# Log-sum-exp on one core: regrouping the exponentials and row sums of the first five loads

## The chip, the cores and the metric

The kernel runs on one core of a Trainium2 chip. The metric is the time of one execution on the device in microseconds (us), lower is better; the median of several runs is compared. The engines that matter here are ScalarE (ACT), which computes the exponentials, VectorE (DVE), which adds rows up, SyncE (SP), which issues the loads and stores, and the 16 DMA engines behind SP's queue.

## The reference

```python
x = np.random.randn(32, 512, 1024).astype(np.float32)

def reference(x):
    max_x = np.max(x, axis=-1, keepdims=True)
    return (max_x.squeeze(-1) + np.log(np.sum(np.exp(x - max_x), axis=-1))).astype(np.float32)
```

That is a stable log-sum-exp over the last axis: 16,384 rows of 1,024 numbers, 67 MB read, 64 KB written.

## The kernel before

The 16,384 rows are spread over 128 partitions, 128 rows in each. "A row" below means one row in each partition, 1,024 float32 columns (0.5 MB over all partitions). The kernel takes the exponential without subtracting the maximum, sums it and takes the logarithm; a check at the end (the matmuls into `count`, L143 to L251) decides whether the sums stayed in a safe range, and only if not does a second, slower pass run (L258 to L301).

The data come in 18 loads of the sizes in the table `LOADS` (L17), from 16 rows down to 0.375. They go into a ring of 48 rows (`RING`) in the on-chip memory, one after the other; when a load would run past the end, the position goes back to 0. Loads 1 to 3 fill the 48 places, load 4 (16 rows) overwrites load 1, load 5 (13.5) begins at place 16, load 6 (12.5) at 29.5, and load 7 (9) begins again at 0.

The function `load` issues a load on SP's queue (L126). Before it does, SP waits for every earlier user of the places that it overwrites; `users` holds those with the engine and the count at which they are done, and an entry that has been waited for is dropped. SP issues in the order of the loads. The loads carry no wait for each other, so several can be under way in the queue.

Each load has a string of operations that work through its rows in order:

- `Rn`: one exponential over n rows on ACT, in place (L192), then one row sum of these n rows on DVE (`reduce_sum`, L196).
- `Tn`: one exponential over n rows on ACT (L192), then on DVE for each row one `scalar_tensor_tensor` that adds its two halves and accumulates the sum (L204).
- `A`: one row on ACT alone, exponential and sum in one instruction with an accumulator (L181).
- `Y`, `Z`: the two pieces of the last row, on ACT with an accumulator (L170).

The last operation of a load also takes the exponential of the part of a row that the load ends with, so that the next load finds it done (`upto`, L190).

ACT waits for a load to land and then runs its operations without a wait for DVE. DVE waits for each exponential. The only wait of ACT for DVE before the tail is at row 119 (`LATE`), before the early logarithm (L219) over rows 0 to 111, which by then have been summed. Both engines run in the order in which the program is written.

Of the kernel before, what the change touches and what calls it, by code (L numbers as in the profile page):

```python
# [14 lines left out]


LOADS = [  # L17
    (16, "R8 R7 A"), (16, "R8 R7 T1"), (16, "R8 R8"), (16, "R6 R5 R5"), (13.5, "R5 R4 T4"),
    (12.5, "R7 R6"), (9, "A A A A A A A A A"), (7.5, "R3 R2 R2"), (5.5, "R4 T2"),
    (4.625, "T4"), (3.3125, "T3"), (2.4375, "T3"), (1.8125, "T2"), (1.3125, "T1"), (0.9375, "T1"),  # L20
    (0.5625, "T1"), (0.625, "Y"), (0.375, "Z"),
# [341 lines left out]
```

## Time and profile before

| | |
|---|---|
| median of 3 runs | 162.66 us (162.47 to 162.76) |
| the profiled execution | 163.04 us, of which the span of the profile is 161.7 us |
| busy: DMA queue / DVE / ACT | 97.2% / 73% / 72% of the span |
| read from HBM | 67.11 MB, 415 GB/s over the span |

A row of the profile's groups reads: line, engine, operation, what it writes <- what it reads with shapes, count | busy us in all, mean ns of one | idle time of the engine just before these, and what ended most of it. A row of a timeline reads: start, duration (both us from the start of the span), engine, line, operation, count when several that follow each other are merged, and in brackets the idle time before it and who ended it. "SPq" is SP's queue of instructions, where the issue of a load is seen. A row of the DMA issues gives the size in KB and the time from the issue to the landing.

### The profile page before, as it was taken

What the parts mean: (1) busy time and instruction counts of PE and PEld (TensorE: products, weight loads), DVE (VectorE), ACT (ScalarE), POOL (GpSimd) and SP (SyncE); (2) the same over time, 40 slices, a digit from 0 to 9 for tenths busy, and PEclk for the clock granted to TensorE, in tenths of its full rate; (3) what the DMA queues carried; (4) which work ended last, traced back from release to release, by engine and by line L of the source; (5) the groups of instructions that cost most, each with busy time, mean ns of one, the idle gap of its engine ahead of it and who ended that gap; (6) DMA issues with size and microseconds to landing.
All of it is one profiled execution on the core that took longest, in us unless ns stands there. A gap on an engine that the chain in (4) does not pass through costs nothing.

```text
span 161.7 us, 249 instructions
## 1 busy us (share of the span) xinstructions
PE 2.1 (1%) x24; PEld 1.0 (1%) x24; DVE 117.7 (73%) x69; ACT 116.9 (72%) x55; POOL 0.2 (0%) x4
## 2 busy tenths in 40 slices
PE   0000000000000000000000000000000000000022
PEld 0000000000000000000000000000000000000011
DVE  0000000899929999399999999999399956999894
ACT  3000059980899609994299949973999999989986
POOL 0000000000000000000000000000000000000000
DMA  7997997998999899799699999998999999999990
GB/s 276 503 519 324 454 519 324 454 519 373 405 519 422 357 519 454 324 519 454 284 438 438 438 422 405 443 494 368 438 438 441 410 417 418 450 408 418 410 392 15
DMA packets 2881, 67.18 MB, mean 416 GB/s; under 512 B 576, under 2 KB 704, under 8 KB 1344
## 3 DMA queue, kind: packets, MB, share of 16 engines
q1 hardware_dynamic: 2880, 67.18, 97.2%
q14 instruction: 1, 0.01, 0.0%
HBM read 67.11 MB, written 0.07 MB: 415 GB/s over the span
## 4 chain that ended last, share of the span: by engine, by line
DMA 58%; ACT 19%; DVE 16%; another core or an unknown queue 3%; SPq 1%; issue 0%; PE 0%; DVEq 0%
DMA ring<-in_x_dram 58%; ACT ring L192 19%; DVE sumexp L196 15%; DVE ring L204 1%; SPq L126 0%; PE count L147 0%; PE count L248 0%; DVE clamped L242 0%; DVE fine L251 0%; SPq L44 0%; DVEq L44 0%
## 5 line engine op out<-in xcount | busy, mean ns | idle before, releaser
L192 ACT ACTIVATE ring<-ring 128x8192 f32<-128x8192 f32 (+18 forms) x27 | 103.6, 3891 | 41.8 <-DMA ring<-in_x_dram 41.8
L196 DVE TENSOR_REDUCE sumexp<-ring 128x8 f32<-128x8192 f32 (+6 forms) x17 | 102.9, 6107 | 39.2 <-ACT ring L192 39.2
L204 DVE SCALAR_TENSOR_TENSOR ring<-ring 128x512 f32<-128x512 f32 x22 | 14.1, 687 | 1.3 <-ACT ring L192 1.3
L181 ACT ACTIVATE ring<-ring 128x1024 f32<-128x1024 f32 x10 | 10.4, 1042 | 0.0
L114 ACT ACT_TABLE_LOAD x1 | 1.3, 1283 | 1.5 <-PEq L57 1.5
L143 PE MATMUL count<-far,bad 128*1 128x1 f32 x2 | 0.2, 164 | 153.8 <-DVE clamped L138 153.8
L181 ACT ACTIVATION_READ_ACCUMULATOR ring<-ring 128x1 f32 x10 | 1.9, 187 | 0.0
L204 DVE DVE_READ_ACCUMULATOR ring<-ring 128x1 f32 x22 | 1.8, 82 | 0.0
L147 PE MATMUL count<-sumexp,ones 128*1 128x1 f32 x20 | 1.8, 164 | 4.1 <-DVE ring L204 4.1
L170 ACT ACTIVATE last_exp<-ring 128x640 f32<-128x640 f32 (+1 forms) x2 | 1.2, 590 | 0.0
L115 DVE MEMSET ones<- 128x1 f32 x1 | 0.1, 59 | 1.5 <-PEq L57 1.5
L143 PEld LDWEIGHTS count<-far,bad 128*1 128x1 f32 x2 | 0.1, 80 | 153.8 <-DVE clamped L138 153.8
L147 PEld LDWEIGHTS count<-sumexp,ones 128*1 128x1 f32 x20 | 0.8, 81 | 5.1 <-DVE ring L204 4.9
L251 DVE TENSOR_SCALAR fine<-count 1x1 int32<-1x1 f32 x1 | 0.1, 145 | 0.5 <-PE count L147 0.5
L170 ACT ACTIVATION_READ_ACCUMULATOR last_exp<-ring 128x1 f32 x2 | 0.4, 186 | 0.0
L138 DVE SCALAR_TENSOR_TENSOR clamped<-clamped,sumexp 128x119 f32<-128x119 f32 x1 | 0.3, 282 | 0.0
L232 ACT ACTIVATE res<-sumexp 128x1 f32<-128x1 f32 x1 | 0.3, 294 | 0.0
L219 ACT ACTIVATE res<-sumexp 128x112 f32<-128x112 f32 x1 | 0.3, 279 | 0.0
L242 DVE SCALAR_TENSOR_TENSOR clamped<-sumexp 128x9 f32<-128x9 f32 x1 | 0.2, 169 | 0.1
L133 DVE TENSOR_SCALAR clamped<-sumexp 128x119 f32<-128x119 f32 x1 | 0.2, 223 | 0.0
L230 ACT ACTIVATE res<-sumexp 128x15 f32<-128x15 f32 x1 | 0.2, 198 | 0.0
L248 PE MATMUL count<-far,bad 128*1 128x1 f32 x2 | 0.2, 164 | 0.0
(8 smaller groups left out, 0.7 us busy)
## 6 DMA issues: line engine op xcount, KB each, us to landing
ring<-in_x_dram SPq DMA_DIRECT2D x1, 6912.0 KB, 31.8
ring<-in_x_dram SPq DMA_DIRECT2D x1, 6400.0 KB, 26.6
ring<-in_x_dram SPq DMA_DIRECT2D x1, 4608.0 KB, 25.2
ring<-in_x_dram SPq DMA_DIRECT2D x1, 3840.0 KB, 23.6
ring<-in_x_dram SPq DMA_DIRECT2D x1, 2816.0 KB, 26.0
ring<-in_x_dram SPq DMA_DIRECT2D x1, 2368.0 KB, 30.4
ring<-in_x_dram SPq DMA_DIRECT2D x1, 1696.0 KB, 23.1
ring<-in_x_dram SPq DMA_DIRECT2D x1, 1248.0 KB, 25.7
```

Source lines behind the costliest of these rows:

```text
L114: nc.scalar.preload_act_table_set("natural_log_exp_and_others")
L133: dve.did(nc.vector.tensor_scalar(out=clamped[:, 0:LATE], in0=sumexp[:, 0:LATE], scalar1=LOW, scalar2=HIGH, op0=ALU.max, op1=ALU.min,))
L138: dve.did(nc.vector.scalar_tensor_tensor(out=clamped[:, 0:LATE], in0=clamped[:, 0:LATE], scalar=0.0, in1=sumexp[:, 0:LATE], op0=ALU.bypass ...
L143: pe.did(nc.tensor.matmul(count, lhsT=bad[:, 0:1], rhs=far, start=True, stop=False))
L147: return pe.did(nc.tensor.matmul(count, lhsT=ones, rhs=sumexp[:, c : c + 1], **kw))
L170: at = act.did(nc.scalar.activation(out=last_exp[:, here - p : end - p], in_=ring[:, here:end], func=AF.Exp, accum_out=sumexp[:, LAST : NC ...
L181: at = act.did(nc.scalar.activation(out=v, in_=v, func=AF.Exp, accum_out=sumexp[:, c : c + 1]))
L192: at = act.did(nc.scalar.activation(out=v, in_=v, func=AF.Exp))
L196: who = (dve, dve.did(nc.vector.reduce_sum(out=sumexp[:, c : c + s], in_=rows, axis=AX.X)))
L204: who = (dve, dve.did(nc.vector.scalar_tensor_tensor(out=lo, in0=lo, scalar=1.0, in1=rows[:, r, H:d], op0=ALU.mult, op1=ALU.add, accum_out ...
L219: ln_early = act.did(nc.scalar.activation(out=res[:, 0:W], in_=sumexp[:, 0:W], func=AF.Ln))
L232: ln_last = act.did(nc.scalar.activation(out=res[:, LAST:NC], in_=sumexp[:, NC : NC + 1], func=AF.Ln, bias=sumexp[:, LAST:NC]))
```

## The change

The operations of the first five loads are grouped differently; sizes and order of the loads stay as they are. Load 1 becomes one exponential and one row sum over 16 rows, loads 2 to 4 become two of 8 rows each, load 5 becomes 7 and 6 rows. The row that ACT summed alone in load 1 (`A`) and the single rows of loads 2 and 5 (`T1`, `T4`) become part of row sums on DVE. Because `load` waits for whole operations, the moments at which places of the ring come free change with the groups.

```diff
 LOADS = [
-    (16, "R8 R7 A"), (16, "R8 R7 T1"), (16, "R8 R8"), (16, "R6 R5 R5"), (13.5, "R5 R4 T4"),
+    (16, "R16"), (16, "R8 R8"), (16, "R8 R8"), (16, "R8 R8"), (13.5, "R7 R6"),
     (12.5, "R7 R6"), (9, "A A A A A A A A A"), (7.5, "R3 R2 R2"), (5.5, "R4 T2"),
```

## The prediction

> **What bounds the kernel now.** I read the page of the profile first, for the totals: which engine or queue is full.
>
> ```profile
> span 161.7 us, 249 instructions
> ...
> PE 2.1 (1%) x24; PEld 1.0 (1%) x24; DVE 117.7 (73%) x69; ACT 116.9 (72%) x55; POOL 0.2 (0%) x4
> ...
> q1 hardware_dynamic: 2880, 67.18, 97.2%
> ```
>
> The load queue is full for 97.2% of the span, while ACT and DVE each stand idle for more than a quarter of it. That points at the transfers. A mean over the span can hide a stage that has another limit, though, so I went to the chain of waits next, the work that ended last followed back.
>
> ```profile
> 41.17 14.04 ACT ring L192 x3
> 55.21 5.29 another core or an unknown queue
> 60.52 7.04 ACT ring L192
> 67.58 17.29 DVE sumexp L196 x2
> 84.95 26.63 DMA ring<-in_x_dram
> ```
>
> At first sight this contradicts the totals: 14.04 us of exponentials and 17.29 us of row sums, exactly the operations that the change regroups, stand on the chain. The chain follows semaphores: it goes from load 6 back to the row sum that released its place in the ring, and from there to load 3. It does not show that load 6, once issued at 84.95, had to queue behind load 5 anyway. Whether it had to is seen by setting two timelines beside each other. First ACT, whose starts after a wait for a DMA are the landings of the loads:
>
> ```profile
> 21.83 7.03 ACT L192 ACTIVATE ring<-ring 128x8192 f32<-128x8192 f32 x1 [19.09 <-DMA ring<-in_x_dram]
> 41.17 14.04 ACT L192 ACTIVATE ring<-ring 128x8192 f32<-128x8192 f32 x3 [5.21 <-DMA ring<-in_x_dram]
> 60.52 13.95 ACT L192 ACTIVATE ring<-ring 128x8192 f32<-128x8192 f32 x2 [5.31 <-DMA ring<-in_x_dram]
> 79.88 14.04 ACT L192 ACTIVATE ring<-ring 128x6144 f32<-128x6144 f32 x3 [5.41 <-DMA ring<-in_x_dram]
> 96.30 11.91 ACT L192 ACTIVATE ring<-ring 128x5120 f32<-128x5120 f32 x3 [2.38 <-DMA ring<-in_x_dram]
> 111.60 10.96 ACT L192 ACTIVATE ring<-ring 128x6656 f32<-128x6656 f32 x2 [3.39 <-DMA ring<-in_x_dram]
> ```
>
> Then SP's queue, the moments at which loads 1, 4, 5, 6, 7, 8, 11 and 15 are issued (loads 2 and 3 follow load 1 at once):
>
> ```profile
> 0.00 0.39 SPq L126 DMA_DIRECT2D ring<-in_x_dram  x1
> 45.18 0.33 SPq L126 DMA_DIRECT2D ring<-in_x_dram  x1
> 64.52 0.33 SPq L126 DMA_DIRECT2D ring<-in_x_dram  x1
> 84.95 0.33 SPq L126 DMA_DIRECT2D ring<-in_x_dram  x1
> 97.25 0.33 SPq L126 DMA_DIRECT2D ring<-in_x_dram  x1
> 108.04 0.33 SPq L126 DMA_DIRECT2D ring<-in_x_dram  x1
> 125.09 0.33 SPq L126 DMA_DIRECT2D ring<-in_x_dram  x1
> 131.49 0.33 SPq L126 DMA_DIRECT2D ring<-in_x_dram  x1
> ```
>
> Loads 2, 3 and 4, of 16 rows each, land 19.34, 19.35 and 19.36 us after the one before. Loads 5 and 6 (13.5 and 12.5 rows) take 16.42 and 15.30; at load 4's 1.21 us per row they would take 16.34 and 15.13. So over loads 2 to 6 the stream of transfers runs at one rate, and at most 0.25 us of it could be a gap. Load 4 is issued 15.3 us before load 3 lands, load 5 15.4 before load 4, load 6 11.35 before load 5, load 7 14.35 before load 6. I call this distance the lead: as long as it covers the start-up of a load, the stream has no hole. The start-up is in the trace: load 1 has nothing ahead of it and lands at 21.83 instead of 19.35, so 2.48 us. That includes whatever a completion costs, so it is an upper bound for the lead needed.
>
> The end of the kernel is therefore set by the stream, and ACT behind it waits 5.2 to 5.4 us for each of loads 2 to 4.
>
> **The change part by part.** The question is: how late do the row sums become, and does a lead fall under 2.48 us? For this I need the price of each operation.
>
> ```profile
> L196 DVE TENSOR_REDUCE sumexp<-ring 128x8 f32<-128x8192 f32 x4 | 34.7, 8684 | 32.9 <-ACT ring L192 32.9
> L192 ACT ACTIVATE ring<-ring 128x8192 f32<-128x8192 f32 x4 | 28.0, 7025 | 29.6 <-DMA ring<-in_x_dram 29.6
> L196 DVE TENSOR_REDUCE sumexp<-ring 128x7 f32<-128x7168 f32 x3 | 22.8, 7612 | 2.6 <-ACT ring L192 2.6
> L204 DVE SCALAR_TENSOR_TENSOR ring<-ring 128x512 f32<-128x512 f32 x22 | 14.1, 687 | 1.3 <-ACT ring L192 1.3
> L192 ACT ACTIVATE ring<-ring 128x5120 f32<-128x5120 f32 x3 | 13.3, 4459 | 2.4 <-DMA ring<-in_x_dram 2.4
> L196 DVE TENSOR_REDUCE sumexp<-ring 128x6 f32<-128x6144 f32 x2 | 13.1, 6547 | 0.4 <-ACT ring L192 0.4
> L192 ACT ACTIVATE ring<-ring 128x7168 f32<-128x7168 f32 x2 | 12.3, 6159 | 0.0
> L181 ACT ACTIVATE ring<-ring 128x1024 f32<-128x1024 f32 x10 | 10.4, 1042 | 0.0
> ...
> 28.89 16.21 DVE L196 TENSOR_REDUCE sumexp<-ring 128x8 f32<-128x8192 f32 x2 [27.28 <-ACT ring L192]
> 117.38 14.08 DVE L196 TENSOR_REDUCE sumexp<-ring 128x7 f32<-128x7168 f32 x2 [2.65 <-ACT ring L192]
> 134.67 5.55 DVE L196 TENSOR_REDUCE sumexp<-ring 128x3 f32<-128x3072 f32 x2 [3.21 <-ACT ring L192]
> ```
>
> One more row of a sum costs 8.684 - 7.612 = 1.072 us; back to back, 8 and 7 rows take 16.21 and not 16.30, so each following operation saves a seam of 0.085. A sum over 16 rows is not in the trace; by the slope it is 8.684 + 8 x 1.072 = 17.26, and by two separate sums of 8 at most 17.37; I take 17.26. An exponential over 16 rows goes by the slope from 5120 to 8192 elements, 0.835 ns per element: 7.025 + 6.84 = 13.87. Two of 8 rows would be 14.05.
>
> What the regrouping adds: one row of load 1 moves from ACT (L181, 1.04) to DVE (+1.07), and five rows of loads 2 and 5 move from L204 (0.687) to the row sum (1.072), +0.385 each, 1.9 together. DVE gets about 3.0 us more work, ACT a little less. The larger effect is the order: DVE now starts on load 1 after the whole exponential, not after half of it.
>
> Row sums, start to end: load 1 lands at 21.83, exponential to 35.70, sum to 52.99 (from 35.73; today DVE starts at 28.89). From here DVE finds its input always ready. Load 2's exponentials end at 48.2 and 55.2, load 3's at 67.6 and 74.5, load 4's at 86.9 and 93.9, load 5's at 102.5 and 108.2, load 6's unchanged at 117.4 and 122.6; the closest is 86.9, with DVE free for it at 87.4. So DVE runs on in steps of 8.60 (8 rows), 7.53 (7 rows) and 6.46 (6 rows): load 2 ends at 61.59 and 70.19, load 3 at 78.79 and 87.39, load 4 at 95.99 and 104.59, load 5 at 112.12 and 118.58, load 6 at 126.11 and 132.57.
>
> Issues, 0.08 us after the sum that frees the place (as today, 45.10 to 45.18). The ring has 48 places, so load 4 overwrites load 1's 16 rows, load 5 takes the 13.5 places from 16, load 6 those from 29.5, and load 7 starts again at 0. Load 4 goes out at 53.07 (today 45.18), lead 60.52 - 53.07 = 7.45. Load 5 needs both halves of load 2: 70.27, lead 9.6. Load 6 reaches to place 42, into the second half of load 3: 87.47, lead 8.8. Load 7's 9 rows now need both halves of load 4: 104.67 (today 97.25), lead 111.60 - 104.67 = 6.9. Load 8 follows load 5's seven rows, 112.20; for its lead, the landing of load 7:
>
> ```profile
> ring<-in_x_dram SPq DMA_DIRECT2D x1, 4608.0 KB, 25.2
> ```
>
> That load is issued at 97.25 today and lands at 122.45, so load 8's lead is 10.25. Loads 9 and 10 go out by 118.7, load 11 at 126.2 instead of 125.09 and load 15 at 132.65 instead of 131.49. SP does nothing else that these waits could hold up: it issues in order, and the results' stores come behind load 18.
>
> The smallest lead is 6.9 us against 2.48 needed, 4.4 to spare. So every landing stays where it is, and ACT, which is never made to wait by DVE before its early logarithm, keeps its times from load 2 on. DVE had been idle 3.21 us until 134.67, when load 8's first exponential is done; it now arrives at 132.57, 2.1 to spare. From there on the two kernels do the same work on the same dates. What is moved later is covered by the stream, what is saved on ACT goes into its wait for the next load, and the sum of the change is 0 within the 0.25 us that the stream's own irregularity leaves.
>
> A rule speaks against the regrouping. The Trainium skill, Trace Analysis, section Optimizing Scalar/DVE Operations, says that where these engines are not saturated but cause bubbles elsewhere, breaking instructions up can let work finish sooner; that is the opposite of what is done here. The trace has the engines at 72% and 73%, so the rule's first condition holds; its second, a bubble, needs a lead under the start-up, and the sum has none. The Trainium skill, DMA: Bandwidth & Descriptors, section Latency and other measured facts, puts a hardware queue's first byte at about 0.6 us, so by that the spare is wider than by the 2.48 of load 1.
>
> The profiled execution has 163.04 us for a span of 161.7, so 1.34 lie around the span, and it is 0.38 above the median of 162.66. With a sum of 0 the forecast is 163.04 for an execution profiled like that one, and 162.66, rounded 162.7, for the median.
>
> **The rivals.** First, slower: the queue runs short. All leads of loads 4 to 8 (6.9 to 10.25) will be shorter than the shortest that the trace shows free of cost, 11.35. If the queue needs more than 2.48 us to go over from one load to the next without a hole, the first to show it is load 7; it decides from a lead of 6.9 up, or from DVE being more than 4.4 us later than worked out. One hole costs between nothing and one start-up, 2.48: up to 165.1; all five would be 12.4, 175.1. Against it speaks that load 1's start-up is measured and that a lead of 11.35 shows no more gap than one of 15.4. I give it 0.14, most of it at small prices.
>
> Second, slower: DVE is late for the tail. It has no idle time left from 35.7 to 132.6; if the sum over 16 rows, or the chain of ten others, takes over 2.1 us longer than worked out, DVE misses load 8 at 134.67, and what is more than the small idle times behind that comes out at the end. A sum 5 us too long would give about 165. The sums of 8 rows agree too well for that: 0.03.
>
> Third, faster: fewer operations on the chain. If the chain were the limit, ACT's saving would count: load 1's three exponentials (7.025 + 6.159 + 1.042 = 14.23) against 13.87, and 14.04 against 13.95 (load 2 beside load 3) for each of loads 2, 4 and 5, together 0.63 us, 162.0. By the Trainium skill, the same section of Trace Analysis, grouping helps where an engine is saturated, at about 93 ns per ScalarE instruction; the five exponentials saved would be an estimated 0.47 us, 162.2. Against it: the 5.2 to 5.4 us that ACT waits for the loads. All that is to be won in this stretch is the 0.25 us that loads 5 and 6 take above load 4's rate: 162.4, inside what counts as no change. 0.07.
>
> **How the numbers follow.** No change: 0.76. About 0.2% (0.33 us) is what a measurement of this kernel can tell from no change, so that is 162.33 to 162.99, and the first two rivals make 0.17 slower, the third 0.07 faster. The range takes the band of no change and reaches up to 163.3, into the rival of a partly paid start-up (about 0.05); it leaves out the faster case and the full prices.
>
> **What would show it.** Right: the row sum over 16 rows takes about 17.3 us; load 4 is issued near 53.1 and load 7 near 104.7; the landings stay at 41.2, 60.5, 79.9, 96.3 and 111.6; DVE waits about 2 us before load 8's first sum at 134.7. Wrong: a landing that slips against the one before, at load 7 above all, with a larger wait of ACT on the DMA; or no idle time of DVE at 134.7 and ACT or the last sums later than today.

## The result and the profile after

| | before | changed |
|---|---|---|
| median, 22 runs each, side by side | 162.70 us | 162.43 us |
| ratio to before | | 0.9984, interval 0.9978 to 0.9990 |
| profiled execution / its span | 163.04 / 161.7 us | 162.54 / 161.2 us |

The changed kernel is 0.27 us faster. That is small, and lies within the 0.33 us that the prediction counted as no change, but with 22 runs on each side it is clear of the noise. The page of the changed kernel:

```profile
span 161.2 us, 227 instructions
...
PE 2.1 (1%) x24; PEld 1.0 (1%) x24; DVE 120.4 (75%) x57; ACT 116.2 (72%) x49; POOL 0.2 (0%) x4
...
q1 hardware_dynamic: 2880, 67.18, 97.3%
q14 instruction: 3, 0.02, 0.0%
```

The last row is the instruction queue. The prediction did not show this row of the kernel before, which is:

```profile
q14 instruction: 1, 0.01, 0.0%
```

DVE has 2.7 us more work, nearly the 3.0 forecast, and 12 instructions fewer in the trace (69 to 57). The timeline of ACT in the changed kernel gives the landings (start, duration, operation, idle time before it):

```profile
22.09 13.86 ACT L192 ACTIVATE ring<-ring 128x16384 f32<-128x16384 f32 x1 [19.35 <-DMA ring<-in_x_dram]
41.42 13.95 ACT L192 ACTIVATE ring<-ring 128x8192 f32<-128x8192 f32 x2 [5.47 <-DMA ring<-in_x_dram]
60.78 13.95 ACT L192 ACTIVATE ring<-ring 128x8192 f32<-128x8192 f32 x2 [5.41 <-DMA ring<-in_x_dram]
80.13 13.95 ACT L192 ACTIVATE ring<-ring 128x8192 f32<-128x8192 f32 x2 [5.40 <-DMA ring<-in_x_dram]
96.47 11.81 ACT L192 ACTIVATE ring<-ring 128x7168 f32<-128x7168 f32 x2 [2.40 <-DMA ring<-in_x_dram]
111.61 10.96 ACT L192 ACTIVATE ring<-ring 128x6656 f32<-128x6656 f32 x2 [3.32 <-DMA ring<-in_x_dram]
151.17 6.60 ACT L192 ACTIVATE ring<-ring 128x2496 f32<-128x2496 f32 x5
```

Up to load 6 the landings stand where they stood, within 0.3 us. The last row is new: five exponentials of the tail run without a break. In the kernel before, ACT stops in the middle of these five and waits for load 13. That row, from its timeline, with the transfers of the instruction queue between 151.5 and 153 us beside it, and then the same queue in the changed kernel between 159.3 and 160.8:

```profile
154.10 4.48 ACT L192 ACTIVATE ring<-ring 128x1856 f32<-128x1856 f32 x4 [0.53 <-DMA ring<-in_x_dram]
q14 instruction: 1, 0.01, 1.3%
```

```profile
q14 instruction: 1, 0.01, 1.4%
```

One transfer of 8 KB, by the queue's name code for an engine, starts at 152.17 us in the kernel before, in the middle of the loads, and none does in the changed kernel until 159.83, when all loads have landed (from the trace's list of transfers). A second one follows in both kernels at the very end (161.80 and 161.08), and the third packet of the changed kernel has 24 bytes; neither of these two is meant below. Load 13 then lands 2.90 us after load 12 before the change and 2.25 after it. At 1.21 us per row its 1.8125 rows should take 2.2 us.

The chain of waits of the changed kernel, for how little it says of cost:

```profile
35.98 82.78 DVE sumexp L196 x9
...
118.78 25.18 DMA ring<-in_x_dram
...
157.77 1.34 ACT last_exp L170 x4
```

Half the span is now put down to DVE's row sums, and the kernel is faster. The 25.18 us of load 10 are almost wholly time in the queue behind others, as for load 6 in the chain before.

### The profile page after: what moved, and what is told of

Same layout as the page of the kernel before. It is cut to its first block, busy times and chain, and to the rows that moved or that the text cites. A ratio compares the mean times of both kernels' runs of the same rounds, so it can differ in the third digit from the quotient of the medians.

```text
span 161.2 us, 227 instructions
## 1 busy us (share of the span) xinstructions
PE 2.1 (1%) x24; PEld 1.0 (1%) x24; DVE 120.4 (75%) x57; ACT 116.2 (72%) x49; POOL 0.2 (0%) x4
## 4 chain that ended last, share of the span: by engine, by line
DVE 51%; DMA 29%; ACT 16%; issue 2%; PE 0%
DVE sumexp L196 51%; DMA ring<-in_x_dram 29%; ACT ring L192 15%; ACT last_exp L170 1%; ACT res L219 0%; PE count L147 0%; DVE fine L251 0%
## 5 line engine op out<-in xcount | busy, mean ns | idle before, releaser
L196 DVE TENSOR_REDUCE sumexp<-ring 128x8 f32<-128x8192 f32 (+6 forms) x15 | 108.8, 7326 | 36.3 <-ACT ring L192 36.3
L192 ACT ACTIVATE ring<-ring 128x8192 f32<-128x8192 f32 (+15 forms) x23 | 103.8, 4571 | 41.8 <-DMA ring<-in_x_dram 41.8
L204 DVE SCALAR_TENSOR_TENSOR ring<-ring 128x512 f32<-128x512 f32 x17 | 10.7, 689 | 0.6 <-ACT ring L192 0.6
L181 ACT ACTIVATE ring<-ring 128x1024 f32<-128x1024 f32 x9 | 9.4, 1041 | 0.0
```

Of the source, the lines that this page charges most:

```text
L181: at = act.did(nc.scalar.activation(out=v, in_=v, func=AF.Exp, accum_out=sumexp[:, c : c + 1]))
L192: at = act.did(nc.scalar.activation(out=v, in_=v, func=AF.Exp))
L196: who = (dve, dve.did(nc.vector.reduce_sum(out=sumexp[:, c : c + s], in_=rows, axis=AX.X)))
L204: who = (dve, dve.did(nc.vector.scalar_tensor_tensor(out=lo, in0=lo, scalar=1.0, in1=rows[:, r, H:d], op0=ALU.mult, op1=ALU.add, accum_out ...
```

## The experiments

Four theories. **F, fetch:** the code transfer at 152 us holds up one of the 16 DMA engines; a load has landed when the slowest engine is done, so load 13 and all after it are late; the trace shows one landing of the 16 behind the others, but does not name the engine. The change takes instructions from DVE, and with them moves the transfer behind the loads. **S, stream:** loads 5 and 6 run at the full rate (16.34 and 15.13 us instead of 16.42 and 15.30), the only gain that the prediction saw. **N, noise.** And later **G, grouping:** fewer and larger operations are worth the time themselves.

**The kernel before, again.** No edit.

> The kernel before, unchanged, for a second profile. Theory F (fetch): the two profiles differ by one 8 KB transfer of the instruction queue, at 152.2 us in the kernel before, in the middle of the loads, and at 159.8 in the changed one, after them; it holds up one DMA engine, so that load 13 and all later loads land 0.6 to 0.8 us late. F expects the fetch near 152 again and load 13 landing more than 2.5 us after load 12 (2.90 in the first profile, 2.25 in the changed kernel). Theory S (stream): loads 5 and 6 of the kernel before take 16.42 and 15.30 us instead of 16.34 and 15.13, because something disturbs single packets there; S expects these two numbers again. Theory N (noise): both are accidents of one execution; N expects other numbers in this profile. All expect a ratio of 1.000.

Measured: ratio 0.9999 (0.9990 to 1.0008). The timeline of ACT, and the instruction queue between 151.5 and 153 us:

```profile
80.01 14.04 ACT L192 ACTIVATE ring<-ring 128x6144 f32<-128x6144 f32 x3 [5.39 <-DMA ring<-in_x_dram]
96.36 11.91 ACT L192 ACTIVATE ring<-ring 128x5120 f32<-128x5120 f32 x3 [2.30 <-DMA ring<-in_x_dram]
111.49 5.75 ACT L192 ACTIVATE ring<-ring 128x6656 f32<-128x6656 f32 x1 [3.22 <-DMA ring<-in_x_dram]
153.66 4.43 ACT L192 ACTIVATE ring<-ring 128x1856 f32<-128x1856 f32 x4 [0.33 <-DMA ring<-in_x_dram]
q14 instruction: 1, 0.01, 1.4%
```

S falls: loads 5 and 6 take 16.35 and 15.13 us here, without any change. The 0.25 us belonged to one execution. The wait for load 13 and the transfer (152.13) are there again, as F expected, but load 13 lands 2.72 us after load 12 and not 2.90.

**The changed kernel, again.** No edit.

> The changed kernel, unchanged, for a second profile and time. F: fetch near 159.8, after the loads, loads 12 to 13 take 2.25 us, 0.27 us faster than the kernel before. S: loads 5 and 6 take 16.34 and 15.13 again, the same 0.27 us. N: ratio nearer 1.000 than 0.9984 and other numbers in the profile.

Measured: ratio 0.9989 (0.9980 to 0.9998), transfer at 159.62, load 13 lands 2.25 us after load 12. N falls with it: the gain repeats, if a little smaller.

**Twelve instructions given back to DVE.**

```diff
     dve.did(nc.vector.memset(far, 100 * HIGH))
+    pad = sbuf("pad", 32)
+    for j in range(12):
+        dve.did(nc.vector.memset(pad[:, j : j + 1], 1.0))
```

> The changed kernel with 12 memsets of one column on DVE at its start, where DVE waits 34 us for data anyway; DVE then executes as many instructions as in the kernel before (57 to 69). Everything else stays. F, if it is DVE's code that is fetched: the fetch is back near 152, load 13 lands 0.6 to 0.8 us later, and the time goes back to the kernel before's (ratio 1.000). F, if it is ACT's code: fetch stays near 159.8 and the time at 0.998. S and N: no change against the changed kernel, 0.998.

Measured: ratio 1.0006 (0.9997 to 1.0015), the gain is gone. From its page, its instruction queue between 151.5 and 153 us and the timeline of ACT:

```profile
PE 2.1 (1%) x24; PEld 1.0 (1%) x24; DVE 120.9 (75%) x69; ACT 116.3 (72%) x49; POOL 0.2 (0%) x4
q14 instruction: 1, 0.01, 1.4%
153.86 4.47 ACT L195 ACTIVATE ring<-ring 128x1856 f32<-128x1856 f32 x4 [0.48 <-DMA ring<-in_x_dram]
```

The grouping is that of the change, the early operations and loads are those of the change, and yet the transfer is back at 152.12, load 13 comes late by nearly as much (2.86 us after load 12), and the time is that of the kernel before. Twelve memsets of some 60 ns, executed some 34 us before DVE's first sum, decide it.

**Six instructions given back to ACT.** The same with `act.wait(dve, 1)` and six exponentials of one column.

> The changed kernel with 6 exponentials of one column on ACT at its start, where ACT waits 19 us for load 1; ACT then executes as many instructions as in the kernel before (49 to 55). F, if it is ACT's code that is fetched: fetch back near 152, load 13 late, ratio 1.000. F, if it is DVE's code: fetch near 159.8, ratio 0.998. S and N: 0.998.

Measured: ratio 0.9989 (0.9980 to 0.9998), transfer at 159.51. So it is DVE's number of instructions that moves the transfer, not ACT's.

**The early grouping kept, eight DVE instructions taken out; and the late grouping with four put in.** The first edits the kernel before, the second is the changed kernel with four memsets as above.

```diff
-    (16, "R8 R7 A"), (16, "R8 R7 T1"), (16, "R8 R8"), (16, "R6 R5 R5"), (13.5, "R5 R4 T4"),
+    (16, "R8 R7 A"), (16, "R8 R7 R1"), (16, "R8 R8"), (16, "R6 R5 R5"), (13.5, "R5 R4 R4"),
```

> The kernel before with its early grouping, only the five single rows of loads 2 and 5 summed as row sums (T1 to R1, T4 to R4). DVE executes 8 instructions fewer (69 to 61), each exponential and each wait of the loads stays as before. F: the number of DVE instructions alone decides; if 8 fewer are enough, the code fetch moves from 152 to near 159.6, behind the loads, load 13 lands 2.25 us after load 12, and the ratio is 0.998 to 0.999, as that of the changed kernel. If 8 are not enough, the fetch stays near 152 and the ratio is 1.000. Rival G (grouping): the gain comes from the fewer, larger exponentials and sums of loads 1 to 4; G expects 1.000 whatever the fetch does.

> The changed kernel with 4 memsets of one column on DVE at its start: 61 DVE instructions, as many as in the kernel before with its single rows as row sums. F expects the same place of the fetch as there, and the time that goes with it: 0.998 to 0.999 if it is near 159.6, 1.000 if near 152. G expects 0.998 to 0.999 whatever the fetch does.

Measured: 0.9995 (0.9987 to 1.0004) and 1.0002 (0.9993 to 1.0011). I had expected the transfer at one of the two known places. It came at a third: the instruction queue of either kernel between 156.5 and 158 us, and ACT in the second:

```profile
q14 instruction: 1, 0.01, 1.5%
```

```profile
q14 instruction: 1, 0.01, 1.4%
158.47 0.71 ACT L173 ACTIVATE last_exp<-ring 128x640 f32<-128x640 f32 x1 [0.94 <-DMA ring<-in_x_dram]
```

At 157.09 and 156.80 it is still among the loads. It spares load 13 (2.26 us after load 12 in both). In the first kernel load 18 lands 0.47 us late behind load 17, in the second load 17 lands 0.95 us late, and ACT waits 0.94 us for it. Two quite different groupings with the same number of DVE instructions have the transfer in the same place and times that cannot be told apart.

**Load 7 issued later.** This is about the prediction's rule for leads, not about the gain. The changed kernel with one more wait of SP before load 7:

```diff
         for a, b, who, at in users:
             if a < here + size and b > here:
                 sp.wait(who, at)
+        if i == 6:
+            sp.wait(act, 9)      # the other kernel: sp.wait(dve, 10)
```

> The changed kernel, but SP issues load 7 only when ACT is done with load 5's exponentials, near 108.35 instead of 104.8 us: a lead of about 3.1 us before load 6 lands, instead of 6.8. The prediction's rule (a lead over the start-up of 2.48 us makes no hole): load 7 lands 10.9 us after load 6 as before, and the time is that of the changed kernel. Its first rival (a lead shorter than those seen costs up to 2.48 us): load 7 lands up to 2.5 us late and the time is up to 2.5 us more.

> The changed kernel, but SP issues load 7 only when DVE is done with load 5's first sum, near 112.25 us, 0.8 us after load 6 has landed. The prediction's rule: the stream stands for 2.48 us from the issue, so load 7 lands 0.8 + 2.48 less the completion that a start-up and a landing share, 2.3 to 3.3 us late, all later loads with it, and the time is 2.3 to 3.3 us more than that of the changed kernel, near 165.

Measured: 0.9991 (0.9982 to 1.0000) and 1.0176 (1.0161 to 1.0190), 162.56 and 165.58 us. The issue of load 7 on SP's queue in either kernel, and ACT's first row of load 7 in the second:

```profile
108.15 0.33 SPq L128 DMA_DIRECT2D ring<-in_x_dram  x1
```

```profile
112.15 0.33 SPq L128 DMA_DIRECT2D ring<-in_x_dram  x1
125.51 1.06 ACT L183 ACTIVATE ring<-ring 128x1024 f32<-128x1024 f32 x1 [3.17 <-DMA ring<-in_x_dram]
```

Load 6 lands at 111.36 in both. A lead of 3.2 us costs nothing that the time shows: load 7 lands 11.02 us after load 6, 0.1 more than elsewhere. An issue 0.79 us too late moves the landing by 3.21 us (14.13 after load 6 instead of 10.92), of which 2.42 are the start-up, against 2.48 read off load 1. All later loads and the end move with it.

**One, two and three instructions given to DVE.** The changed kernel with so many memsets; the aim was a place between the last load and the last store.

> The changed kernel with 1 memset on DVE at its start (58 instructions). So far the code fetch came at 152.1 us with 69 DVE instructions, near 157.0 with 61 and near 159.6 with 57, where it holds up not a load but one engine's part of the last store: its last landing is 0.30 to 0.41 us behind the one before it, 0.04 to 0.05 where the fetch came earlier. F expects a place in between for 58 to 60; after the last load (158.0) and before the store's packets (from about 160) it would cost neither, and the kernel would end some 0.3 us earlier than the changed one, ratio 0.997. Before 158 it costs as at 157: 0.9995 to 1.000. Rival (the place of the fetch has nothing to do with the end): 0.9985 to 0.999 as the changed kernel.

> The same with 2 memsets (59 DVE instructions). F: as with 1; a fetch between 158.1 and 159.3 gives 0.997, one before 158 gives 0.9995 to 1.000, one near 159.6 gives 0.9985 to 0.999.

> The same with 3 memsets (60 DVE instructions), the nearest to the 61 with which the fetch came near 157. F: most likely a fetch between 157.0 and 158.0 and 0.9995 to 1.000; if it falls after 158.1, 0.997.

Measured: 0.9979 (0.9971 to 0.9988), 0.9979 (0.9970 to 0.9988) and 0.9997 (0.9988 to 1.0006). With one and two the transfer stays at 159.57 and 159.68, with three it is at 156.85. There is no place in between to be had this way. One instruction more, the third, brings 0.24 us back (162.31 to 162.55): in that kernel ACT waits for the last load again.

```profile
158.64 0.49 ACT L173 ACTIVATE last_exp<-ring 128x384 f32<-128x384 f32 x1 [0.29 <-DMA ring<-in_x_dram]
```

**Both kernels without the body of the second pass.** These data never enter it; both kernels leave out lines 262 to 301, so that DVE's code is shorter and has no branch at the end.

> The changed kernel without the body of its second pass, which these data never enter (the range check stays, but nothing would follow from it): DVE then has neither the body nor the branch over it, and runs straight to its end. F: the fetch at 159.6, which goes with that branch, is gone; the last store's landings lie within 0.05 us again instead of 0.3, and the kernel ends up to 0.3 us earlier than the changed one, ratio 0.996 to 0.998. Rival (that fetch costs nothing): 0.9985 as the changed kernel, apart from a shorter way of ACT past the body.

> The kernel before without the body of its second pass, in the same way. G (grouping): it stays behind the changed kernel without that body by as much as before, 0.15%. F: if DVE's shorter code needs no fetch among the loads any more, load 13 lands 2.25 us after load 12 and the two kernels end within 0.1% of each other; if the fetch at 152 is still there, load 13 is late by 0.4 to 0.8 us and the difference stays.

Measured: 0.9984 (0.9975 to 0.9994) and 0.9996 (0.9987 to 1.0005). Two misses. I had tied the transfer at 159.6 to the branch of DVE; without any branch it is still there, at 160.23, behind DVE's last operation, in the changed kernel (its timeline of DVE, and the instruction queue between 159.3 and 160.8):

```profile
159.80 0.15 DVE L251 TENSOR_SCALAR fine<-count 1x1 int32<-1x1 f32 x1 [0.55 <-PE count L147]
q14 instruction: 1, 0.01, 2.0%
```

And in the kernel before it stays at 152.04, with load 13 again 2.90 us after load 12. So neither the body nor the branch behind sets the place. The number of DVE's instructions moves it, but not to one fixed count: in the first group of the table below the transfer starts when DVE has begun 44 of its 69 instructions (during the second of load 12's three row sums), in the second group at 53 of 61 or 52 of 60 (during load 14's row sum), in the third after all 57 to 59. Neither kernel was freed of the transfer, so the grouping without any transfer was not measured.

All runs by the place of the transfer; lateness is the last of a load's 16 landings less the third-last, in us, from the trace. Place and lateness are those of the one profiled execution of each kernel:

```
transfer at      kernel                      load 13  load 18  last store  ratio to before
152.0 to 152.2   before                        0.85     0.82      0.04      1
                 before, again                 0.48     0.37      0.05      0.9999
                 changed + 12 DVE              0.81     0.78      0.04      1.0006
                 before, no second pass        0.68     0.66      0.05      0.9996
156.8 to 157.1   before, rows for singles      0.10     0.55      0.05      0.9995
                 changed + 4 DVE               0.07     0.99      0.05      1.0002
                 changed + 3 DVE               0.08     0.66      0.04      0.9997
159.5 to 160.3   changed                       0.36     0.35      0.31      0.9984
                 changed, again                0.15     0.15      0.32      0.9989
                 changed + 6 ACT               0.10     0.10      0.30      0.9989
                 changed, lead 3.2             0.15     0.14      0.41      0.9991
                 changed + 1 DVE               0.11     0.11      0.24      0.9979
                 changed + 2 DVE               0.22     0.23      0.34      0.9979
                 changed, no second pass       0.28     0.31      0.29      0.9984
```

The lateness is not the transfer's alone: in the changed kernel some 0.35 us stand from load 1 on, and in the kernel before load 12 already has 0.22. What the transfer adds is read off the distance of two landings. Load 13 lands 2.72 to 2.90 us after load 12 in the first group and 2.25 to 2.27 in all others, so it is 0.47 to 0.65 us late; in the second group load 17 or 18 is 0.47 to 0.95 us late in the same sense.

The seven ratios with the transfer behind the loads (0.9979 to 0.9991) and the six measured with it among them (0.9995 to 1.0006) do not overlap, though some of their intervals do. Within a place the grouping makes no difference: at 152 the old one has 0.9996 and 0.9999 and the new one 1.0006; at 157 the old one has 0.9995, the new ones 0.9997 and 1.0002. So the new grouping gains nothing where the transfer stays among the loads, and G falls, to within about 0.1%. All seven kernels with the transfer behind the loads have the new grouping; the old one was never brought there, so a gain that needs both is not excluded.

## Why the prediction was wrong

**Right: the dates of the early part.** Load 4 was issued at 53.23 (53.07 forecast), load 5 at 70.48 (70.27), load 6 at 87.65 (87.47), load 7 at 104.83 (104.67). The rows in the changed kernel, SP's queue first, then DVE:

```profile
53.23 0.33 SPq L126 DMA_DIRECT2D ring<-in_x_dram  x1
70.48 0.33 SPq L126 DMA_DIRECT2D ring<-in_x_dram  x1
87.65 0.33 SPq L126 DMA_DIRECT2D ring<-in_x_dram  x1
104.83 0.33 SPq L126 DMA_DIRECT2D ring<-in_x_dram  x1
```

```profile
35.98 17.22 DVE L196 TENSOR_REDUCE sumexp<-ring 128x16 f32<-128x16384 f32 x1 [34.36 <-ACT ring L192]
134.68 3.35 DVE L196 TENSOR_REDUCE sumexp<-ring 128x3 f32<-128x3072 f32 x1 [1.94 <-ACT ring L192]
```

The sum over 16 rows takes 17.22 (17.26), and DVE waits 1.94 us before load 8's first sum (2.1). The landings held, and the start-up as the bound for a lead was borne out by the two later issues. In the prediction's own rows the load with the shortest lead, load 6 (11.35 us), took 0.17 us more than the rate gives (15.30 against 15.13); the repeat of the kernel before has 15.13, so the lead was not the reason. The first two rivals, a queue that runs short and a late DVE, fall.

**Wrong: the sum of 0.** The step that failed is "From there on the two kernels do the same work on the same dates." The operations are the same, but the loads of the tail are not on the same dates: load 13 came 0.65 us late behind load 12 in the kernel before (0.47 in its repeat), and those after it with it. The place of the code transfer, which the change moves, was a term that the sum did not have. Three readings led there. The rate of the stream was checked over loads 2 to 6 alone and then taken for all 18; the same division at load 13, 2.90 us where 2.2 are the rate, would have shown the hole. The chain of waits was quoted only up to load 6; its end, shown here, goes through the landing of load 13 at 154.08, and the prediction passed over it.

```profile
125.94 28.14 DMA ring<-in_x_dram
154.08 0.02 issue
154.10 3.92 ACT ring L192 x3
```

And the page's row of the instruction queue was overlooked; its one packet had a date, and the windows of the DMA view would have given it.

**Wrong, and by chance near: the third rival.** It put what could be won at 0.25 us, 162.4, and 162.43 was measured. But it named the irregularity of loads 5 and 6, which the repeat of the kernel before does not have. The size is a coincidence. Its other reading, ACT's saved operations on the chain, falls with the runs by place.

**The missing term.** The change takes five single-row sums and two row sums from DVE, 12 instructions in the trace. The transfer moves from 152.2 to 159.8; in the profiled pair the last load lands at 158.24 instead of 158.99, 0.75 us earlier; in the repeated pair it is 158.03 instead of 158.49, 0.46 us earlier. Of the 0.75 the spans keep 0.5, and in the medians 0.27 us remain: the transfer now stands beside the last store, whose last landing is 0.31 us behind the third-last, where it was 0.04. From the last load's landing to the last store's it is 2.87 to 3.04 us in the seven kernels with the transfer there and 2.41 to 2.68 in the others. That the transfer is what delays the store is only argued; no kernel was found in which it meets neither the loads nor the store. The changed kernel with one or two memsets more had the lowest ratio (0.9979), but its interval overlaps that of the changed kernel, so it isn't shown to be better.

The Trainium skill, Runtime: NRT & Kernel Launch, section Instruction fetch mechanics, says that a sequencer fetches the next page of its code through a DMA queue of its own while it executes the current one, and that this is mostly hidden. The first part agrees with the traces (the instruction queue, next to DVE's count). Hidden it is for DVE, which shows no gap, and not for the loads, one of which lands 0.47 to 0.95 us late.

Open: what decides at which of DVE's instructions the transfer starts, and why three memsets move it by 2.8 us while two don't move it; and why the same 8 KB, which take 0.31 to 0.37 us among the loads, make a load 0.47 to 0.95 us late.

## What to carry to other kernels

In a kernel that is bound by its loads, list every transfer that shares the DMA engines with them, the instruction queue's too, and give each a date; here a single one of 8 KB delayed all loads that landed after it. Check the rate of a stream over its whole length, load by load, before calling two kernels' tails the same. When a change alters the number of instructions, a change of a few tenths of a microsecond is tested by giving the instructions back as idle ones before crediting the change itself.

## What was not expected of the hardware

A transfer of 8 KB that takes 0.31 to 0.37 us itself among the loads made the load it fell on land 0.47 to 0.95 us late. The landing that had fallen behind caught up little in the full stream: it was 0.85 us behind at load 13 and still 0.82 at load 18 in the kernel before, 0.48 and 0.37 in its repeat. The transfer's place moved with DVE's number of instructions: with 60, 61 and 69 it came among the loads, with 57, 58 and 59 behind them. Six more instructions on ACT didn't move it, nor did taking the branch out of DVE's code.
